# Storing q and k whole and splitting them beside the attention, with one plain gate moved ahead of the seven-product pairs

## The chip, the cores and the metric

The kernel runs on one core of one Trainium2 chip. The metric is device time in microseconds for one execution on that core; the kernel before was run three times, and its median is the number to beat. One further execution was taken with the hardware profiler, and every row quoted below is from it. Engines are named as the profile names them: PE is the matrix engine (PEld its weight loads), DVE the vector engine, ACT the scalar engine, POOL is GpSimd, SP the engine that issues most of the DMAs.

## The reference

One decoder block over 1024 tokens of width 1024, all in float32:

```python
h = rms_norm(x, g_pre_mix)
z = h @ w_in                 # q, k, v (1536 each), glu_in (2048), z_ga, z_gc (1024 each)
y_attn = dilated_attention_mixer(q, k, v, rel_bias_table, w_attn_out)
y_conv = conformer_conv_mixer(glu_in, ...)   # GLU, causal 31-tap depthwise conv, LayerNorm, swish, matmul
merged = sigmoid(z_ga) * y_attn + sigmoid(z_gc) * y_conv
x = x + rms_norm(merged @ w_mix_out, g_post_mix)
x = x + rms_norm(swiglu_ffn(rms_norm(x, g_pre_ffn), w_ffn_in, w_ffn_out), g_post_ffn)
```

The attention has three groups of eight heads (head size 64). A group with dilation d lets a token attend itself and up to 128 earlier tokens at distance d, with a learned bias by distance; the three groups' outputs are merged by their softmax denominators. A query block's score is `q . k / 8 + bias`.

## The kernel before

**Split products.** A float32 matrix product is made from rounded parts: an operand x becomes hi (x rounded to the matrix engine's format) and lo = x - hi, and a product is hi*hi + hi*lo + lo*hi, three matmuls of 128 x 512 per 128 rows of depth. hi is a copy on ACT, lo a subtraction on DVE or POOL (`wsplit` names which; it is changed from stage to stage).

**Units and pairs.** A *unit* (L288) is one 128 x 512 output at full depth: 24 matmuls. A *plain gate* is two units over the same weights. A *seven-product pair* (`winograd`, L316) makes four such outputs from two weight blocks with seven half-depth products of 12 matmuls each, 84 instead of 96; for it the weights are summed in four combinations (`quarters`, L191, steps 0 to 5: steps 1 and 3 are additions, the others splits), and the activations likewise, once (`quarter_sums`, L353). The outputs that need more than one product are taken from PSUM in callbacks f11, f12, f21, f22; the first, third and fourth products are copied out by ACT (L325, L330, L335), since their bank goes on accumulating or is summed with another.

**Order.** The program is written out in order by Python for all engines; each engine runs its own list in that order and waits on data. Every two or three matmuls a *tick* (L113) lets background generators emit a step: pieces of the weight splits, the convolution, normalisations. A *beat* (L131), one for each matmul of a unit or of v, lets the attention generator advance RATE steps (0.33 while v is made, 0.66 afterwards). Four such advances make one attention step (one block of 128 queries for two heads); eight steps make a head pair, twelve head pairs the attention.

**Stages.** (1) Start, and FIRST = 4 GLU blocks as units, with the quarter sums of the activations beside the last of them; what is not finished of them is forced at the first pair (L315, L336). (2) Pairs: 4 GLU, 4 of gate a, 3 of gate c, 12 of k with q. The depthwise convolution runs beside them on DVE, in PSUM banks of its own: 46 steps for each of 8 channel blocks, spaced by `CONV` (a list of ticks to skip after each step; L677, and another list for the q and k pairs, L1329). (3) v as plain products, with the LayerNorm of the convolution and then the attention beside. (4) LATE = 2 plain gates, the last two blocks of gate c (L1357), stored without their sigmoid, which follows at L1390. (5) The convolution's output product `co`, 16 units; its operand is loaded and split by `conv_split` (L1146), 8 splits for each half of the tokens, the first 8 of which must be out before the first unit (L1366). The rest of the attention and its merges run beside (4) and (5). (6) Attention output, mix, the FFN, its output.

**q and k.** `qk_pair` (L750) takes a pair of outputs, 128 channels (two heads) of k and of q. Every half (512 tokens) is brought into the group's order, split into hi and lo (`parts`, L772: a copy on ACT, L775 or L778, and a subtraction on DVE, L776 or L779; f21 does the same at L797 and L798), and stored to DRAM with one DMA for each part and head, 16 a pair (L769, L681). `stacks` (L805) loads a head's k as hi over lo on 128 partitions, and q's hi and lo on 64 each; `double` (L821) copies them to the other 64 partitions on POOL. A score block is then two matmuls (L967): both contract k's hi and lo in one go, once with q's hi in both halves and once with q's lo. `stacks` is called for the next head pair after the second step of the current one, and `double` after its sixth and seventh.

**Around a step.** In `attention` (L902) the scores of step s are followed by the exponentials of step s-1 on ACT (L980), the transposes of step s-3 on PE (L1003) with their split on ACT and DVE (L1008, L1009), and the products with v of step s-4 (L1024, L1026). v is split by `value_parts` (L854) in the third and fourth step.

Of the kernel before, what the change touches and what calls it, by code (L numbers as in the profile page):

```python
# [9 lines left out]
F32 = mybir.dt.float32  # L10
# [29 lines left out]
LATE = 2  # L40
# [18 lines left out]
class Build:  # L59
    def __init__(self, ctx, tc, aps):  # L60
# [12 lines left out]
        self.wsplit = self.nc.vector  # L73
# [117 lines left out]
    def quarters(self, i, c):  # L191
# [13 lines left out]
        elif c == 1:  # L205
            self.s12 = self.slot()
            add(self.s12[:, l], a21, a22, op=OP.add)
# [108 lines left out]
    def winograd(self, W, T, f11, f12, f21, f22):  # L316
# [18 lines left out]
        nc.scalar.copy(v1, V)  # L335
# [414 lines left out]
    def qk_pair(self, g, hp, job):  # L750
# [12 lines left out]
        def out(dst, part, hf, t):  # L763
            for h in range(2):
                d, x = dst[h][part * 64:part * 64 + 64], t[h * 64:h * 64 + 64]
                if dil == 1:
                    self.half_out(d, hf, x)
                else:
                    nc.sync.dma_start(d.rearrange("p (c h m) -> p c h m", c=dil, h=2)[:, :, hf],  # L769
                                      x.rearrange("p (c m) -> p c m", c=dil))  # L770

        def parts(y, hf, dst, scale):  # L772
            h = self.half(F32R)
            if scale is None:
                nc.scalar.copy(h, y)  # L775
                nc.vector.tensor_tensor(y.bitcast(F32R), y, f(h), op=OP.subtract)  # L776
            else:
                nc.scalar.activation(h, y, AF.Copy, scale=scale)  # L778
                nc.vector.scalar_tensor_tensor(y.bitcast(F32R), y, scale, f(h), op0=OP.mult, op1=OP.subtract)  # L779
            out(dst, 0, hf, f(h))  # L780
            out(dst, 1, hf, y)

        def row1(hf):
            def g(z, x):
                y = self.half()
                nc.vector.tensor_tensor(perm(y), nat(z), nat(x), op=OP.add)
                return lambda: parts(y, hf, dk, None)
            return g

        def f22(x, v):  # L790
            y = self.half()
            nc.vector.tensor_tensor(perm(y), nat(x), nat(v), op=OP.add)
            return lambda: parts(y, 1, dq, 0.125)

        def f21(x):
            h, l = self.half(F32R), self.half(F32R)
            nc.scalar.activation(perm(h), nat(x), AF.Copy, scale=0.125)  # L797
            nc.vector.scalar_tensor_tensor(perm(l), nat(x), 0.125, perm(f(h)), op0=OP.mult, op1=OP.subtract)  # L798
            out(dq, 0, 0, f(h))
            out(dq, 1, 0, f(l))  # L800
# [1033 lines left out]
```

## Time and profile before

| | |
|---|---|
| median of 3 runs | 1761.38 us (1760.35 to 1761.72) |
| the profiled execution | 1763.24 us |
| its span, first to last instruction | 1761.4 us |
| granted clock of the matrix engine, mean | 0.991 |
| bytes moved by DMA | 274.93 MB |

The median stands within a tenth of a per cent of the profiled execution. Busy time is the sum over instructions of an engine; on PE, where matmuls overlap, a row's mean duration (0.39 us for 128 x 512) is longer than the time from one start to the next. An idle entry in square brackets or behind the last bar of a group tells what the engine waited for just before the instruction. `out<-in` names tiles without their numbers: b are the 4 KB slots, c the 2 KB halves, p a PSUM bank. In the waits, `PE p L311 <- ACT c L325: 9.3, 2, 8.1` reads: PE at line 311 waited 9.3 us in all, in 2 places, 8.1 at the longest, for what ACT wrote at line 325.

### The profile page before, as it was taken

The page shows a single profiled execution, that of the slowest core. Times are in us where ns is not written, and L with a number is a line of the kernel's source. Part 1 is how long each engine was busy: PE and PEld are TensorE (multiplying, and loading weights), DVE is VectorE, ACT ScalarE, POOL GpSimd, SP SyncE. Part 2 cuts the span into 40 slices and gives each one's busy share as a digit, 9 for nine tenths or more (in the row PEclk, how much of TensorE's full clock was granted, in tenths as well). Part 3 has the DMA queues.
Part 4 walks back from the last instruction along what each step waited for, and adds up shares of the span by engine and source line. Part 5 has one row for each costly group of instructions (what it writes and reads, how often), then busy time and mean ns, then how long its engine had stood idle before and what let it go on. Part 6 is the DMA issues. An engine that isn't in the chain of part 4 may idle for free.

```text
span 1761.4 us, 24497 instructions
## 1 busy us (share of the span) xinstructions
PE 1714.6 (97%) x8698; PEld 1454.6 (83%) x8698; DVE 1245.9 (71%) x2207; ACT 792.3 (45%) x1549; POOL 478.5 (27%) x348
## 2 busy tenths in 40 slices
PE   8989999999999999999889999999999999999998
PEld 6768888888877999998678888878888888888886
DVE  6879988899896666556785675585665565667686
ACT  6333444444443576556542245633333333354453
POOL 0017778788774132233210130040000000000000
PEclk9989999999999999999899999999999999999999
DMA  4332433566667696669943742213233223395234
GB/s 161 123 133 102 138 131 126 148 191 170 166 166 196 220 283 163 170 185 273 280 155 120 275 164 87 102 39 123 90 121 113 90 103 113 132 337 178 97 129 150
DMA packets 185782, 274.93 MB, mean 156 GB/s; under 512 B 56113, under 2 KB 107948, under 8 KB 185660
## 3 DMA queue, kind: packets, MB, share of 16 engines
q1 hardware_dynamic: 185020, 272.74, 48.8%
q8 instruction: 68, 1.11, 0.3%
q10 hardware_dynamic: 576, 0.56, 0.1%
q14 instruction: 54, 0.44, 0.1%
q0 software_dynamic: 64, 0.07, 0.0%
HBM read 183.76 MB, written 94.28 MB: 158 GB/s over the span
## 4 chain that ended last, share of the span: by engine, by line
PE 84%; DVE 5%; DMA 4%; ACT 3%; issue 2%; POOL 1%; SPq 1%; DVEq 0%; ACTq 0%; POOLq 0%
PE p L311 13%; PE p L312 13%; PE p L313 13%; PE p L1718 12%; PE p L1452 5%; PE p L299 4%; PE p L295 4%; PE p L297 4%; PE p L885 2%; PE p L883 2%; PE p L887 2%; PE p L524 2%; PE p L967 2%; DMA b<-w_in 1%; PE p L1003 1%
## 5 line engine op out<-in xcount | busy, mean ns | idle before, releaser
L311 PE MATMUL p<-b,b 128*128 128x512 f32 x1204 | 470.8, 391 | 9.9 <-ACT c L325 9.3
L313 PE MATMUL p<-b,b 128*128 128x512 f32 x1204 | 470.5, 391 | 3.9 <-POOL b L188 3.9
L312 PE MATMUL p<-b,b 128*128 128x512 f32 x1204 | 470.1, 390 | 0.0
L311 PEld LDWEIGHTS p<-b,b 128*128 128x128 f32 x1204 | 226.9, 188 | 58.9 <-ACT c L325 10.3
L313 PEld LDWEIGHTS p<-b,b 128*128 128x128 f32 x1204 | 227.0, 189 | 52.9 <-POOL b L188 5.7
L312 PEld LDWEIGHTS p<-b,b 128*128 128x128 f32 x1204 | 227.1, 189 | 47.3
L187 ACT CAST b<-b 128x1024 fp32r<-128x1024 f32 x129 | 135.6, 1051 | 199.2 <-POOL b L208 73.4
L1718 PE MATMUL p<-b,b 128*128 128x512 f32 x924 | 209.6, 389 | 0.0
L1718 PEld LDWEIGHTS p<-b,b 128*128 128x128 f32 x924 | 173.4, 188 | 36.0
L188 POOL TENSOR_TENSOR b<-b,b 128x1024 fp32r<-128x1024 f32 x69 | 167.3, 2425 | 129.9 <-ACT b L187 117.6
L651 DVE SCALAR_TENSOR_TENSOR p<-b,par,p 128x511 f32<-128x511 f32 (+14 forms) x232 | 163.4, 737 | 0.0
L188 DVE TENSOR_TENSOR b<-b,b 128x1024 fp32r<-128x1024 f32 x60 | 73.4, 1223 | 127.3 <-ACT b L187 127.3
L295 PE MATMUL p<-b,b 128*128 128x512 f32 x368 | 150.5, 409 | 0.0
L299 PE MATMUL p<-b,b 128*128 128x512 f32 x368 | 148.9, 405 | 0.0
L297 PE MATMUL p<-b,b 128*128 128x512 f32 x368 | 148.8, 404 | 0.0
L885 PE MATMUL p<-b,b 128*128 128x256 f32 x384 | 114.0, 297 | 1.1 <-DVE b L181 1.1
L883 PE MATMUL p<-b,b 128*128 128x256 f32 x384 | 113.3, 295 | 0.0
L887 PE MATMUL p<-b,b 128*128 128x256 f32 x384 | 112.7, 293 | 0.0
L1086 DVE TENSOR_TENSOR b<-c,b 128x512 fp32r<-128x512 f32 x101 | 71.3, 706 | 40.5 <-ACT b L1085 40.1
L1086 DVE TENSOR_TENSOR b<-b,b 128x512 fp32r<-128x512 f32 x117 | 84.7, 726 | 17.3 <-ACT b L1085 15.3
L1085 ACT CAST b<-b 128x512 fp32r<-128x512 f32 x117 | 72.1, 619 | 44.5 <-PE p L1718 13.1
L1452 PE MATMUL p<-b,b 128*128 128x512 f32 x384 | 88.9, 391 | 0.0
(222 smaller groups left out, 2991.4 us busy)
## 6 DMA issues: line engine op xcount, KB each, us to landing
b<-w_in SPq DMA_DIRECT2D x53, 512.0 KB, 4.7
b<-w_fi SPq DMA_DIRECT2D x44, 512.0 KB, 4.7
dk<-c SPq DMA_DIRECT2D x96, 128.0 KB, 2.5
dq<-c SPq DMA_DIRECT2D x96, 128.0 KB, 2.4
b<-dq SPq DMA_DIRECT2D x48, 256.0 KB, 8.8
b<-dk SPq DMA_DIRECT2D x24, 512.0 KB, 7.6
dqS<-c SPq DMA_DIRECT2D x44, 256.0 KB, 2.2
b<-w_fo SPq DMA_DIRECT2D x44, 256.0 KB, 5.4
```

Of the source, the lines that this page charges most:

```text
L188: self.wsplit.tensor_tensor(lo, x, f(hi), op=OP.subtract)
L295: nc.tensor.matmul(ps, hi[:, s], a, start=kt == 0, stop=False)
L297: nc.tensor.matmul(ps, hi[:, s], b, start=False, stop=False)
L299: nc.tensor.matmul(ps, lo[:, s], a, start=False, stop=kt == nk - 1)
L311: nc.tensor.matmul(ps, hi[:, s], a, start=first and kt == 0, stop=False, skip_group_check=True)
L312: nc.tensor.matmul(ps, hi[:, s], b, start=False, stop=False, skip_group_check=True)
L313: nc.tensor.matmul(ps, lo[:, s], a, start=False, stop=kt == 3, skip_group_check=True)
L651: nc.vector.scalar_tensor_tensor(A[i][:, j:], src[i][:, :H - j], w[i], A[i][:, j:], op0=OP.mult, op1=OP.add)
L885: nc.tensor.matmul(o, a, lo[:, s], start=False, stop=False)
L1086: nc.vector.tensor_tensor(s[:, 512:512 + n], src, f(s[:, :n]), op=OP.subtract)
L1452: nc.tensor.matmul(banks[tt][nh], st, wt[:, nh * H:(nh + 1) * H], start=bool(kt == 0 and a), stop=bool(kt == KT - 1 and b))
L1718: nc.tensor.matmul(acc[t], x, y, start=first and e == 0, stop=last and e == 2, skip_group_check=True)
```

## The change

It has two parts and some settings around them.

*q and k.* `qk_pair` stores each half as it is, in float32, one DMA for both heads (4 a pair instead of 16). The factor 1/8 of q is applied in the callbacks and in the copy at L335. `stacks` loads k's 64 rows of a head twice, into both halves of a tile, and q's likewise (four DMAs a head instead of three). The new `parts` makes the operands for one head and one half of the tokens: ACT copies q (rounding it) to a second tile, POOL subtracts to leave q's lo; POOL rounds the upper half of k in place, rounds the lower half to a spare tile, and subtracts it from the lower half. It is called four times for a head pair, after the fourth to seventh step of the one before; `stacks` is called after the first step. For the first head pair the four calls stand 20 to 38 advances into the wait for the LayerNorm, which has at least 40 now.

*Gates.* LATE is 1 and EARLY is 1: gate c's last block is made as a plain gate after the GLU units and before the first pair; the number of pairs stays.

*Settings.* The first additions of the weight sums (`quarters`, step 1) go to an engine of their own, `wadd`, which is DVE at first, POOL beside the GLU and gate pairs, and DVE from the q and k pairs on; the second additions (step 3) stay with `wsplit`. The convolution keeps its first spacing through the q and k pairs. `conv_split` loads 4 halves ahead instead of 5.

```diff
-LATE = 2
+LATE = 1
+
+EARLY = 1
...
-        self.wsplit = self.nc.vector
+        self.wsplit = self.wadd = self.nc.vector
...
             self.s12 = self.slot()
+            add = self.wadd.tensor_tensor
             add(self.s12[:, l], a21, a22, op=OP.add)
...
-    def winograd(self, W, T, f11, f12, f21, f22):
+    def winograd(self, W, T, f11, f12, f21, f22, scale=1.0):
...
-        nc.scalar.copy(v1, V)
+        nc.scalar.activation(v1, V, AF.Copy, scale=scale)
...
-        def out(dst, part, hf, t):
-            for h in range(2):
-                d, x = dst[h][part * 64:part * 64 + 64], t[h * 64:h * 64 + 64]
-                if dil == 1:
-                    self.half_out(d, hf, x)
-                else:
-                    nc.sync.dma_start(d.rearrange("p (c h m) -> p c h m", c=dil, h=2)[:, :, hf],
-                                      x.rearrange("p (c m) -> p c m", c=dil))
-
-        def parts(y, hf, dst, scale):
...
+        def out(dst, hf, t):
+            if dil == 1:
+                self.half_out(dst, hf, t)
             else:
...
+                nc.sync.dma_start(dst.rearrange("p (c h m) -> p c h m", c=dil, h=2)[:, :, hf],
+                                  t.rearrange("p (c m) -> p c m", c=dil))
...
                 nc.vector.tensor_tensor(perm(y), nat(z), nat(x), op=OP.add)
-                return lambda: parts(y, hf, dk, None)
+                out(dk, hf, y)
...
-            nc.vector.tensor_tensor(perm(y), nat(x), nat(v), op=OP.add)
-            return lambda: parts(y, 1, dq, 0.125)
+            nc.vector.scalar_tensor_tensor(perm(y), nat(x), 0.125, nat(v), op0=OP.mult, op1=OP.add)
+            out(dq, 1, y)
...
-            h, l = self.half(F32R), self.half(F32R)
-            nc.scalar.activation(perm(h), nat(x), AF.Copy, scale=0.125)
-            nc.vector.scalar_tensor_tensor(perm(l), nat(x), 0.125, perm(f(h)), op0=OP.mult, op1=OP.subtract)
-            out(dq, 0, 0, f(h))
-            out(dq, 1, 0, f(l))
+            y = self.half()
+            nc.scalar.activation(perm(y), nat(x), AF.Copy, scale=0.125)
+            out(dq, 0, y)
...
         for h in range(2):
-            k, a, b = self.slot(F32R), self.slot(F32R), self.slot(F32R)
-            nc.sync.dma_start(f(a[top]), dq[h][top])
-            nc.sync.dma_start(f(b[low]), dq[h][low])
-            nc.sync.dma_start(f(k), dk[h])
-            ops.append((k, a, b))
+            k, q = self.slot(F32R), self.slot(F32R)
+            for x, d in ((q, 1), (k, 0)):
+                for r in (slice(0, 64), slice(64, 128)):
+                    nc.sync.dma_start(f(x[r]), self.d_qk[g, hp][d][h * 64:h * 64 + 64])
+            ops.append([k, None, q])
...
-    def double(self, p, hf):
...
+    def parts(self, p, h, c):
+        nc = self.nc
+        s, top, low = slice(c * H, (c + 1) * H), slice(0, 64), slice(64, 128)
+        o = p[2][h]
+        if c == 0:
+            o[1] = self.slot(F32R)
+        k, a, q = o
+        nc.scalar.copy(a[:, s], f(q[:, s]))
+        nc.gpsimd.tensor_tensor(q[:, s], f(q[:, s]), f(a[:, s]), op=OP.subtract)
+        t = self.half(F32R)
+        nc.gpsimd.tensor_copy(k[top, s], f(k[top, s]))
+        nc.gpsimd.tensor_copy(t[low], f(k[low, s]))
+        nc.gpsimd.tensor_tensor(k[low, s], f(k[low, s]), f(t[low]), op=OP.subtract)
...
-                    while after in self.gens or x is None:
+                    n = 0
+                    while after in self.gens or x is None or cur is None and n < 40:
...
+                        n += 1
+                        if cur is None and n in (20, 26, 32, 38):
+                            self.parts(nxt, n // 6 % 2 ^ 1, int(n > 30))
                         yield 0
-                    if cur is None:
-                        self.double(nxt, 0)
-                        self.double(nxt, 1)
...
-                if u in (6, 7) and nxt:
-                    self.double(nxt, u - 6)
+                if 3 < u < 8 and nxt:
+                    self.parts(nxt, u % 2, int(u > 5))
...
-                if u == 2 and order:
+                if u == 1 and order:
                     nxt = self.stacks(*order.pop(0))
...
-        x = [load(i) for i in range(5)]
+        x = [load(i) for i in range(4)]
...
+    early = [job(w_in[NGC + n]) for n in range(8 - EARLY, 8)]
...
+    def plain_gate(n, job):
+        w = B.weights(job)
+        s = B.slot()
+        for hf in range(2):
+            nc.scalar.copy(s[:, hf * H:(hf + 1) * H], B.unit(w, B.h_rhs(hf), KT))
+        nc.sync.dma_start(B.d_gc[n], s)
+
+    for n in range(EARLY):
+        plain_gate(8 - EARLY + n, early[n])
     B.first_sums(qs)
...
-        B.wsplit = nc.gpsimd
+        B.wsplit = B.wadd = nc.gpsimd
...
-    B.CONV = (1, 1, 0, 1)
+    B.wadd = nc.vector
...
     for n in range(LATE):
...
+        plain_gate(8 - LATE - EARLY + n, late[n])
```

34 lines of the change are left out of this document (7 added, 27 removed).

## The prediction

> **What bounds the kernel now.** I read the totals of the engines first, then busy time by stretches of 44 us, then PE's waits, then PE's timeline at the longest wait, and last the chain of waits.
>
> ```profile
> PE 1714.6 (97%) x8698; PEld 1454.6 (83%) x8698; DVE 1245.9 (71%) x2207; ACT 792.3 (45%) x1549; POOL 478.5 (27%) x348
> ```
>
> PE is busy for 97%, so the kernel can only get shorter where PE runs below its rate. The stretches say where (columns: length, busy us and count for PE, PEld, DVE, ACT, POOL, then granted clock, DMA share, GB/s):
>
> ```profile
> 88.00:132.00 44.00, 35.91 (x145) 28.38 (x145) 34.08 (x50) 17.19 (x27) 6.12 (x4) 0.88 0.37 133
> 132.00:176.00 44.00, 44.00 (x196) 36.44 (x195) 43.54 (x57) 17.52 (x26) 35.05 (x20) 1.00 0.29 102
> ...
> 440.00:484.00 44.00, 43.69 (x192) 35.69 (x192) 39.57 (x49) 18.09 (x27) 35.13 (x20) 1.00 0.62 164
> 484.00:528.00 44.00, 41.75 (x177) 34.03 (x177) 42.52 (x53) 17.85 (x25) 32.89 (x19) 0.96 0.67 166
> ...
> 836.00:880.00 44.00, 35.25 (x198) 29.71 (x197) 31.24 (x100) 24.00 (x82) 10.76 (x14) 0.88 0.95 283
> 880.00:924.00 44.00, 39.52 (x235) 33.23 (x234) 36.22 (x106) 22.67 (x74) 6.78 (x9) 0.96 0.47 153
> ```
>
> An undisturbed stretch of 512-wide products holds 196: 44/196 = 0.2245 us each. By that rate the stretch from 88 lost 51 products, 11.4 us; those from 440 and 484 lost 4 and 19, 5.2 us. The two from 836 mix widths; PE stood idle for 8.75 + 4.48 = 13.2 us in them. Who PE waited for:
>
> ```profile
> PE p L311 <- ACT c L325: 9.3, 2, 8.1
> ...
> PE p L313 <- POOL b L188: 3.9, 3, 2.3
> PE p L967 <- DMA b<-dk: 2.5, 1, 2.5
> ...
> PE p L967 <- POOL b L825: 1.1, 1, 1.1
> ```
>
> The longest is at the first seven-product pair:
>
> ```profile
> 108.06 0.39 PE L313 MATMUL p<-b,b 128*128 128x512 f32 x1
> 116.54 0.80 PE L311 MATMUL p<-b,b 128*128 128x512 f32 x1 [8.09 <-ACT c L325]
> 117.13 0.63 PE L312 MATMUL p<-b,b 128*128 128x512 f32 x1
> ```
>
> PE idles 8.09 us because the copy of the first product (L325) stands in ACT's queue behind the splits of the quarter sums; afterwards a product takes 0.63 instead of 0.39 us, the reduced clock (0.88 over the stretch). In the q and k stage the chain of waits runs for once not through PE:
>
> ```profile
> 443.30 1.67 SPq L769
> ...
> 447.72 4.08 DMA b<-w_in
> 451.88 1.06 ACT b L187
> ...
> 455.37 1.74 POOL b L207
> 457.19 1.30 POOL b L208
> ```
>
> There the weights are late: their load stands on SP behind the strided stores of q and k (L769), then GpSimd makes the sums.
>
> **The early gate.** Moving one plain gate from the late stage ahead of the pairs leaves the product count as it is. Its 48 products are 48 x 0.2245 = 10.8 us of work where PE now waits. The gate adds to the queues in question two splits on ACT and two on DVE and two copies out of PSUM; on ACT that is about 4 x 0.6 = 2.4 us (row L1085 below for a 512-wide copy). 8.09 + 2.4 = 10.5 is just under 10.8, and the sixteen ticks let the last quarter sums be issued before the pair instead of being forced inside it. I take -11 for this (idle and reduced clock together; ends -8, if 3 us of idle stay, and -11.4).
>
> **The q and k stage.** The rows that carry it:
>
> ```profile
> L188 POOL TENSOR_TENSOR b<-b,b 128x1024 fp32r<-128x1024 f32 x69 | 167.3, 2425 | 129.9 <-ACT b L187 117.6 <-issue 12.2
> L208 POOL TENSOR_TENSOR b<-b,b 128x512 f32<-128x512 f32 x23 | 32.5, 1412 | 1.8
> L651 DVE SCALAR_TENSOR_TENSOR p<-b,par,p 128x511 f32<-128x511 f32 (+14 forms) x232 | 163.4, 737 | 0.0
> L776 DVE TENSOR_TENSOR c<-c,c 128x512 fp32r<-128x512 f32 x24 | 39.3, 1638 | 14.0 <-ACT c L775 13.9
> L779 DVE SCALAR_TENSOR_TENSOR c<-c,c 128x512 fp32r<-128x512 f32 x12 | 13.8, 1154 | 2.0 <-ACT c L778 2.0
> L786 DVE TENSOR_TENSOR c<-p,c 128x512 f32<-128x512 f32 x24 | 22.9, 956 | 2.6 <-issue 2.6
> L798 DVE SCALAR_TENSOR_TENSOR c<-p,c 128x512 fp32r<-128x512 f32 x12 | 11.4, 948 | 0.5 <-ACT c L797 0.5
> L207 DVE TENSOR_TENSOR b<-b 128x512 f32<-128x512 f32 x20 | 13.7, 684 | 0.0
> L661 DVE TENSOR_TENSOR b<-p,c x8: 691/691/693, 170.8 to 545.5; 128x512 f32<-128x512 f32 x8
> ```
>
> Per pair (84 products, 18.9 us) stores fall from 16 to 4, so SP reaches the next weight load sooner, and none of the four waits for a split any more. GpSimd loses two additions, 2 x 1.41 = 2.8 us, exactly the two that end the chain above. DVE loses two subtractions of 1.638, one of 1.154 and one of 0.948 (8.25 us with the three sums of 0.956, L792 taken like L786) and gains the two additions at 0.684 each beside an idle GpSimd or 1.638 beside a busy one (L776 is such an operation, with both inputs in SBUF): 4.2 to 6.1 us. The convolution keeps its faster beat, 6 steps in 8 ticks instead of 4 in 7, so 21 steps in the pair's 28 ticks instead of 16: 3.7 us more at 0.737. Net -0.3 to +1.6 us of DVE per pair. DVE's idle time now is 4.4 us and 1.5 us in the two stretches, 1.9 and 0.6 us per pair, so the additions hide at the low end and cost up to 1.0 us per pair at the high one. The convolution's last block (L661) ends now at 545.5, near the stage's end; its 12 x 16 = 192 steps take 9 pairs at 21. So 0 to +9, taken +1, since at 43.54 of 44 us of DVE (stretch from 132) PE still ran 196 products. The late weights I take as cured: -5 (ends 0 and -5.2). ACT's 36 copies go from here; ACT is at 18 of 44 us, which is worth nothing. If DVE's cover is gone, the next thing late is q's sum, which PE needs before the last product of a pair.
>
> The Trainium skill ("SBUF — State Buffer", section "SBUF: two separate sides") says that DVE and GpSimd hold a shared port pair exclusively for a whole instruction when DVE has two SBUF inputs. Taken to the end, each moved addition would wait out a GpSimd subtraction of 2.425: 2 x 3.1 = 6.2 instead of at most 3.3 us, and the +1 would become 9 x 3.9 = 35, the time 1786. L776's 1.638 against 0.684 shows the effect, with 0.95 us of waiting and not 2.4; I give this end 2 in 100, inside the second rival.
>
> **The attention stage.** Halving the stored bytes happens in the stage before; here each head still reads 1 MB, in four DMAs instead of three. What is new runs on ACT and GpSimd:
>
> ```profile
> L860 POOL TENSOR_TENSOR b<-b,b 128x512 fp32r<-128x512 f32 x24 | 31.5, 1312 | 188.2 <-ACT b L859 149.4 <-PE p L1026 16.0 <-DMA b<-dq 14.8
> L1085 ACT CAST b<-b 128x512 fp32r<-128x512 f32 x117 | 72.1, 619 | 44.5 <-PE p L1718 13.1 <-DVE b L1573 12.6 <-DVE b L377 8.1
> ...
> b<-dq SPq DMA_DIRECT2D x48, 256.0 KB, 8.8
> ```
>
> ```profile
> 635.05 0.61 POOL L825 CAST b<-b 64x512 fp32r<-64x512 f32 x1 [4.32 <-DMA b<-dq]
> ...
> 641.04 0.61 POOL L825 CAST b<-b 64x512 fp32r<-64x512 f32 x1 [4.20 <-DMA b<-dq]
> ...
> 701.43 1.28 POOL L860 TENSOR_TENSOR b<-b,b 128x512 fp32r<-128x512 f32 x1 [16.66 <-ACT b L859]
> ...
> 725.23 1.29 POOL L860 TENSOR_TENSOR b<-b,b 128x512 fp32r<-128x512 f32 x1 [15.20 <-ACT b L859]
> ...
> 851.19 0.60 POOL L825 CAST b<-b 64x512 fp32r<-64x512 f32 x1 [6.30 <-DMA b<-dq]
> ...
> 855.70 0.61 POOL L825 CAST b<-b 64x512 fp32r<-64x512 f32 x1 [2.96 <-DMA b<-dq]
> ```
>
> A head pair takes 725.23 - 701.43 = 23.8 us, a step 3.0. Four calls of the new split cost GpSimd each a subtraction (1.31), two 64-row copies (0.61) and a 64-row subtraction that no row shows (0.61 to 1.31; nearer the first by its size): 3.1 to 3.8 us, 15 at most of 23.8, hidden. ACT gets 4 x 0.62 = 2.5 us of work, hidden too. The wait is what counts: ACT's copy waits for q in order, and behind it stand the exponentials and the copies of the transposed weights, for which PE waits. q is asked for after the first step instead of the second and used after the fourth (first head) and fifth instead of the sixth: 3 steps ahead instead of 4, 9 us against a median landing of 8.8. In quiet stretches nothing waits. Where GpSimd waits today (4.32 + 4.20 and 6.30 + 2.96) ACT will wait 3 us longer: 11.5 and 12.3 us. Exponentials run one step after the scores and transposes three after, so about 6 us are absorbed: 5.5 + 6.3 reach PE, less the 2.5 + 1.1 that PE loses at the same places today, and less some because the second head is asked as far ahead as before. I take +5 (ends 0, all absorbed, and +30, the four waits and 4 x 3.0 passed on whole). The first head pair is split well before its first scores: -1, the wait for L825.
>
> **The late stage.** With one gate less, 16 ticks instead of 32 cover the first eight activation splits; the first comes at tick 10, then one in 4, so two are done instead of six, and six are forced at once ahead of the first convolution-output unit.
>
> ```profile
> ACT b L1085 <- DMA c<-dact: 9.1, 3, 5.5
> ```
>
> ACT waits 9.1 us for these loads today. Forced together, the splits hold ACT until the last load lands; ends 0 (loads are early) and +12 (one landing of 8.8 in full, and 3 for a reduced clock as at 117). I take +4, near the 5.5 of the row less what PE has queued. Against that the second eight splits now come before the merges: -2 of the 13.2 us idle (ends 0 and -13). The 32 advances of the attention that rode on the moved gate (48 products at 0.66 each) ride on two more of the sixteen output units: nothing.
>
> The Trainium skill ("TensorE: Matmul & The Clock Gate", section "What's actually happening") halves PE's clock after an idle window of about 3.4 us; by that a forced wait of 4 costs 2 to 3 more, and one of 3 nothing more. The stretch from 484 shows 0.96 with no listed wait above 2.3, so here shorter gaps are also punished.
>
> **Edits at nothing:** the scale in L335's copy and in q's sum (same instruction and size), the gate's store, one pair of the FFN whose additions move to DVE (2 x 0.684 where DVE is 71% busy).
>
> **Sum:** -11 - 5 + 1 + 5 - 1 + 4 - 2 = -9. The profiled execution took 1763.2 us around a span of 1761.4; it becomes 1754.2. The median of the runs, 1761.4, lies 1.9 below the profiled execution, so 1752.
>
> **Rivals.** (1) *ACT waits for q in order* and passes all on: +30 instead of +5, 1777. It decides from 14 us passed to PE on. For: 8.8 us landing against 9 us of lead, DMA at 0.95 of its time from 836. Against: only two of twelve stacks wait seriously today. (2) *DVE becomes the bound* beside the faster convolution: no -5, +9 instead of +1, 1765. For: 42.52 of 44. Against: 43.54 without loss. (3) *The late stage clears*: no +4 and +5, and 13 instead of 2 of the idle time gone, 1752 - 20 = 1732. For: dact's loads no longer meet the merges. Against: they meet each other. (4) *The early gate only shifts the wait*: the queue it fills is the one PE waits for; no -11, 1763. For: 10.5 against 10.8. Against: the sums are issued over more ticks.
>
> **Numbers.** Forecast 0.50, rivals 0.17, 0.11, 0.15, 0.07. The range 1735 to 1768 leaves out the far half of (3) and most of (1). Its own range for the forecast is 1744 to 1757. What a measurement here can tell is 0.2%, 3.5 us. Faster: the forecast and (3), with a little of (2): 0.68. Within: parts of (2) and (4): 0.12. Slower: (1) and the rest of (2) and (4): 0.20.
>
> **What would show it.** Right: 196 products in every stretch from 88 to 132 with clock 1.00, no wait on L188 in the q and k stage, the convolution's last block near 490. Wrong: PE waiting for the copy of transposed weights or for an exponential where ACT's idle time ends on a DMA of q; DVE near 44 of 44 with PE waiting for q's sum; a long wait at the first output unit. If the first stretch keeps its gap, the largest term falls and with it the forecast.

## The result and the profile after

The changed kernel takes 1790.81 us (median of 4 runs, 1787.94 to 1791.52) against 1761.55 for the kernel before beside it: ratio 1.0159, interval 1.0140 to 1.0178, some 28 us slower where 9 faster was forecast. Its profiled execution took 1791.15 us around a span of 1789.4. First the busy time in the same stretches as before (columns as there), with the totals of the page:

```profile
PE 1729.5 (97%) x8698; PEld 1467.9 (82%) x8698; DVE 1216.2 (68%) x2183; ACT 797.3 (45%) x1561; POOL 561.6 (31%) x420
```

```profile
88.00:132.00 44.00, 42.57 (x186) 34.15 (x185) 33.27 (x50) 18.64 (x30) 4.92 (x3) 1.00 0.45 161
...
440.00:484.00 44.00, 43.13 (x191) 35.39 (x190) 41.61 (x59) 15.69 (x21) 28.00 (x16) 1.00 0.39 122
484.00:528.00 44.00, 43.85 (x194) 36.00 (x193) 20.81 (x23) 14.97 (x21) 28.59 (x15) 1.00 0.46 135
...
836.00:880.00 44.00, 31.25 (x160) 26.74 (x159) 27.15 (x69) 23.91 (x71) 20.50 (x18) 0.77 0.88 231
880.00:924.00 44.00, 39.27 (x225) 33.23 (x223) 30.75 (x103) 24.51 (x87) 31.61 (x32) 0.92 0.69 207
```

The two gains are there. The stretch from 88 has 186 products instead of 145: 41 x 0.2245 = 9.2 us. Those from 440 and 484 have 385 together instead of 369: 3.6 us. DVE is busy for 20.8 of 44 us there, where it was busy for 42.5. The loss shows in the attention: 160 products instead of 198 in the stretch from 836, with the clock at 0.77 instead of 0.88 (products of several widths, so the count is a first sign only). Who PE waited for:

```profile
PE p L1022 <- DVE c L1005: 12.5, 14, 2.2
PE p L1020 <- DVE b L1027: 12.3, 1, 12.3
PE p L1020 <- POOL b L817: 8.0, 1, 8.0
...
PE p L314 <- ACT c L328: 2.9, 2, 1.4
```

The long wait at the first pair (8.1) is gone. New are two long ones and many short ones. In the changed kernel L816 to L821 are the new split, L963 the scores, L966 the addition of the bias into a shared half, L1004 and L1005 the split of the transposed weights, L1020 and L1022 the products with v, L1027 their sum out of PSUM. The many short waits end on DVE's L1005; what DVE waits for, from 640 to 960 us, stands in its own waits (the kernel before has no such row):

```profile
DVE c L1005 <- POOL b L821: 29.1, 13, 4.3
...
DVE c L966 <- POOL b L821: 10.2, 8, 2.2
```

39 us of waiting for the last instruction of the new split, though neither L1005 nor L966 reads anything that it makes. One of these places in the timelines of GpSimd and of DVE (start, us, engine, line):

```profile
821.75 1.29 POOL L817 TENSOR_TENSOR b<-b,b 128x512 fp32r<-128x512 f32 x1
822.98 0.61 POOL L819 CAST b<-b 64x512 fp32r<-64x512 f32 x1
823.65 0.61 POOL L820 CAST c<-b 64x512 fp32r<-64x512 f32 x1
824.34 1.26 POOL L821 TENSOR_TENSOR b<-b,c 64x512 fp32r<-64x512 f32 x1
```

```profile
825.64 0.42 DVE L1005 TENSOR_TENSOR c<-p,c 128x256 fp32r<-128x256 f32 x1 [4.33 <-POOL b L821]
```

GpSimd's subtraction ends at 825.60 and DVE starts at 825.64. What DVE needs is not the result but the place: L1005 writes into a shared half (`c`), and, as I read it, the half that is next in the row of 13 is the spare tile that L820 wrote and L821 reads last. One call of the split takes GpSimd from 821.75 to 825.68, 3.9 us, and four calls follow one another in order, so a half can be held for many microseconds by an engine that is behind. The run own_12 below tests this reading.

The two long waits, in the timeline of ACT:

```profile
633.84 0.62 ACT L816 CAST b<-b 128x512 fp32r<-128x512 f32 x1 [7.14 <-DMA b<-dq]
...
635.35 0.35 ACT L1004 CAST c<-p 128x256 fp32r<-128x256 f32 x1
...
638.09 0.62 ACT L816 CAST b<-b 128x512 fp32r<-128x512 f32 x1 [2.39 <-DMA b<-dq]
...
851.20 1.17 ACT L1081 CAST b<-c 128x512 fp32r<-128x512 f32 x2 [12.12 <-DMA c<-dact]
```

From 626.7 ACT waits in order for q of the second head pair, whose parts are made during the first. Behind it stand exponentials and the copy of the transposed weights (L1004), which ends at 635.7; PE goes on at 635.85. That is PE's 8.0 us; GpSimd's L817, which the row names, ends at the same moment and isn't what PE reads. From 839 ACT waits 12.1 us for the convolution's activation, in the splits forced ahead of the first output unit; DVE's half of these splits (L1082) waits for ACT's, and behind it stands the L1027 that PE waits for: 12.3 us. SP's timeline shows why those loads (L1149) were late:

```profile
822.52 9.56 SPq L1149 DMA_DIRECT2D c<-dact  x2
832.17 1.13 SPq L801 DMA_DIRECT2D b<-dq  x2
833.36 1.23 SPq L801 DMA_DIRECT2D b<-dk  x2
834.63 1.23 SPq L801 DMA_DIRECT2D b<-dq  x2
835.91 1.23 SPq L801 DMA_DIRECT2D b<-dk  x2
...
841.51 8.42 SPq L1149 DMA_DIRECT2D c<-dact  x6
```

SP itself stands at L1149 from 822.5, two loads in 9.6 us, then issues the eight loads of the next head pair (L801), and only at 841.5 the six that ACT needs. Its waits from 780 to 870 us say what it stood for, again a half of DVE's:

```profile
SPq L1149 <- DVE c L1005: 15.2, 4, 9.2
```

### The profile page after: what moved, and what is told of

Read it like the earlier page. It is cut to its first block, busy times and chain, and to the rows that moved or that the text cites. A ratio compares the mean times of both kernels' runs of the same rounds, so it can differ in the third digit from the quotient of the medians.

```text
span 1789.4 us, 24469 instructions
## 1 busy us (share of the span) xinstructions
PE 1729.5 (97%) x8698; PEld 1467.9 (82%) x8698; DVE 1216.2 (68%) x2183; ACT 797.3 (45%) x1561; POOL 561.6 (31%) x420
## 4 chain that ended last, share of the span: by engine, by line
PE 68%; DVE 4%; POOL 2%; ACT 2%; DMA 2%; issue 2%; SPq 0%; DVEq 0%; POOLq 0%; ACTq 0%
PE p L1720 12%; PE p L314 10%; PE p L315 10%; PE p L316 10%; PE p L1454 5%; PE p L302 3%; PE p L300 3%; PE p L298 3%; PE p L880 3%; PE p L882 2%; PE p L878 2%; PE p L963 2%; PE p L999 1%; PE p L1022 1%; PE p L1020 1%
## 5 line engine op out<-in xcount | busy, mean ns | idle before, releaser
L314 PE MATMUL p<-b,b 128*128 128x512 f32 x1204 | 469.0, 390 | 4.7 <-ACT c L328 2.9
L316 PE MATMUL p<-b,b 128*128 128x512 f32 x1204 | 468.5, 389 | 0.0
L315 PE MATMUL p<-b,b 128*128 128x512 f32 x1204 | 468.5, 389 | 0.0
L1720 PE MATMUL p<-b,b 128*128 128x512 f32 x924 | 209.6, 389 | 0.0
L298 PE MATMUL p<-b,b 128*128 128x512 f32 x368 | 153.9, 418 | 0.0
L300 PE MATMUL p<-b,b 128*128 128x512 f32 x368 | 153.2, 416 | 0.0
L302 PE MATMUL p<-b,b 128*128 128x512 f32 x368 | 151.8, 412 | 0.0
L1082 DVE TENSOR_TENSOR b<-c,b 128x512 fp32r<-128x512 f32 x101 | 73.9, 735 | 46.1 <-ACT b L1081 45.8
L1005 DVE TENSOR_TENSOR c<-p,c 128x256 fp32r<-128x256 f32 (+1 forms) x96 | 52.2, 544 | 71.6 <-ACT c L1004 36.8
L1082 DVE TENSOR_TENSOR b<-b,b 128x512 fp32r<-128x512 f32 x117 | 85.2, 730 | 21.2 <-ACT b L1081 19.2
```

Source lines behind the costliest of these rows:

```text
L298: nc.tensor.matmul(ps, hi[:, s], a, start=kt == 0, stop=False)
L300: nc.tensor.matmul(ps, hi[:, s], b, start=False, stop=False)
L302: nc.tensor.matmul(ps, lo[:, s], a, start=False, stop=kt == nk - 1)
L314: nc.tensor.matmul(ps, hi[:, s], a, start=first and kt == 0, stop=False, skip_group_check=True)
L315: nc.tensor.matmul(ps, hi[:, s], b, start=False, stop=False, skip_group_check=True)
L316: nc.tensor.matmul(ps, lo[:, s], a, start=False, stop=kt == 3, skip_group_check=True)
```

## The experiments

The kernels below ran each beside runs of the kernel before on the same chip. Differences below are taken between ratios and turned to time with 1761 us; so the changed kernel stands at +28.0. The theories by letter, as the expectations use them: **L**, the moved gate costs in the late stage what it wins early; **S**, the spare half that GpSimd holds among the shared ones; **Q**, ACT's waits for q in order. Later ones (F, W, P, O, N) are named where they are tried.

| kernel | median us | ratio (interval) | us against before |
|---|---|---|---|
| changed | 1790.81 | 1.0159 (1.0140 to 1.0178) | +28.0 |
| gate_alone | 1750.27 | 0.9939 (0.9922 to 0.9956) | -10.7 |
| gate_back | 1790.86 | 1.0177 (1.0162 to 1.0192) | +31.2 |
| own_spare | 1778.96 | 1.0104 (1.0089 to 1.0119) | +18.3 |
| q_on_pool | 1815.19 | 1.0312 (1.0296 to 1.0327) | +54.9 |
| five_ahead | 1790.22 | 1.0163 (1.0147 to 1.0178) | +28.7 |
| q_later | 1787.55 | 1.0145 (1.0130 to 1.0160) | +25.5 |
| own_all | 1784.42 | 1.0125 (1.0108 to 1.0142) | +22.0 |
| k_short | 1767.79 | 1.0035 (1.0021 to 1.0049) | +6.2 |
| u2_own | 1777.98 | 1.0092 (1.0073 to 1.0111) | +16.2 |
| u2_short | 1758.44 | 0.9988 (0.9978 to 0.9998) | -2.1 |
| k_dve | 1805.84 | 1.0253 (1.0237 to 1.0268) | +44.6 |
| gate_wadd | 1771.15 | 1.0055 (1.0040 to 1.0070) | +9.7 |
| own_12 | 1769.53 | 1.0054 (1.0039 to 1.0069) | +9.5 |
| u2_12 | 1763.90 | 1.0019 (1.0010 to 1.0028) | +3.3 |
| gate_43 | 1776.11 | 1.0091 (1.0074 to 1.0108) | +16.0 |
| gate_45 | 1752.44 | 0.9957 (0.9942 to 0.9972) | -7.6 |
| u2_45 | 1765.17 | 1.0026 (1.0015 to 1.0038) | +4.6 |
| u2_first | 1762.02 | 1.0002 (0.9993 to 1.0012) | +0.4 |

### The two parts of the change apart

*gate_alone*: the kernel before with one plain gate early, and nothing of q and k.

```diff
-LATE = 2
+LATE = 1
+EARLY = 1
...
+    early = [job(w_in[NGC + n]) for n in range(8 - EARLY, 8)]
...
+    for n in range(EARLY):
+        plain_gate(8 - EARLY + n, early[n])
     B.first_sums(qs)
```

> The kernel before with nothing but one plain gate moved from the late stage ahead of the first pair. Theory L: about -9 at the first pair and +20 or more at the output units, 1772 to 1780 us. Theories S and Q: the late stage is as before, 1750 to 1754.

*gate_back*: the changed kernel with both plain gates late.

```diff
-LATE = 1
+LATE = 2
 
-EARLY = 1
+EARLY = 0
```

> The changed kernel with both plain gates in the late stage again (EARLY 0, LATE 2); q and k stay whole in DRAM. Theory L (the late stage lost the gate that covered the loads and splits of the convolution's activations): the 8 us wait at the first pair comes back (about +9), the 12 us wait at the first output unit and the reduced clock after it go (about -20 to -25), so 1775 to 1780 us. Theories S (the spare half that GpSimd holds in the new split makes DVE and ACT wait for GpSimd) and Q (ACT waits in order for the loads of q) do not need the gate: only the +9 comes, about 1800.

The early gate alone wins 10.7 us, and its late stage pays little for it; L falls as a general cause. In the changed kernel the same edit is worth 3.2 at most (the intervals overlap), since there the one late gate leaves ACT with the forced splits (12.1 us on dact), while gate_back shows 1.3 us on dact and loses the time in small waits instead (18.7 us of PE on DVE's L1005, where the changed kernel has 12.5). So the q and k part costs 28.0 + 10.7 = 38.7 us where the prediction had +2 for all that was not the early gate. PE's own times say where: gate_alone and the changed kernel have the same stages in the same order, and from the first product of v to the first of the mix the one takes 454.6 us (558.3 to 1012.9) and the other 493.2 (556.7 to 1049.9), 38.6 more. From the first pair to the first product of v it is 2.5 less (442.6 against 445.1). All that follows looks for these 38.7.

### The spare half

*own_spare*: the spare tile gets two buffers of its own, for which one of the 44 slots goes.

```diff
-NSLOT = 44
+NSLOT = 43
...
-        t = self.half(F32R)
+        self.uid += 1
+        t = self.pool.tile([128, 512], F32R, tag="t", bufs=2, name=f"t{self.uid}")
```

> The changed kernel, but the spare half of the new split comes from two buffers of its own (one 4 KB slot fewer for the rest), so no half that DVE or ACT write next is ever held by GpSimd. Theory S: the waits of DVE on L821 (17 us in all in the late stage) go, 10 to 15 us less, 1776 to 1781. Theory L: at most 3 us less. Theory Q: no change.

*q_on_pool*: q's rounding copy moves from ACT to GpSimd, which makes each call of the split longer there and takes ACT's wait away.

```diff
-        nc.scalar.copy(a[:, s], f(q[:, s]))
+        nc.gpsimd.tensor_copy(a[:, s], f(q[:, s]))
```

> The changed kernel with the rounding copy of q on GpSimd instead of ACT, so ACT never waits for a load of q. Theory Q: the 8 us wait of PE at the start of the second head pair goes, and smaller ones with it, 1778 to 1783. Theory L: only that one wait goes or shrinks, 1782 to 1788. Theory S: GpSimd is longer busy with each half of a head pair and holds the spare half longer, so the waits on it grow, 1790 to 1800.

9.7 us won by the one, 26.9 lost by the other. In q_on_pool PE's wait of 8.0 us is gone, and DVE's wait for the half that L821 frees grows from 29.1 to

```profile
DVE c L1005 <- POOL b L821: 59.7, 17, 13.0
```

A slower GpSimd makes DVE wait longer, as S has it; as the main cause, Q falls.

*own_12*: one own buffer, taken from the shared halves (12 left), with all 44 slots. *gate_43*: the slot's price by itself, on gate_alone.

```diff
-NHALF = 13
+NHALF = 12
...
-        t = self.half(F32R)
+        self.uid += 1
+        t = self.pool.tile([128, 512], F32R, tag="t", bufs=1, name=f"t{self.uid}")
```

```diff
-NSLOT = 44
+NSLOT = 43
```

> The changed kernel with one buffer of its own for the spare tile, taken from the 13 shared halves (12 left), and all 44 slots. Theory S (sharing costs: a half that GpSimd reads last comes round in the row of halves that DVE, ACT and SP take in order): the waits on L821 go as with two own buffers, and without the slot that those cost, 1779.0 - 8 = 1771 (1768 to 1776). Rival N (the number of halves is what is short): twelve are worse than thirteen, 1788 to 1796.

> The early gate alone (1750.3) with 43 slots instead of 44: the price of the slot that the spare tile's own buffers took, apart from anything with q and k. If the 8 us that PE loses more at 120 to 160, 360 to 400 and 1120 to 1200 us with 43 slots are the slot's: 1756 to 1760. If they come with q and k: 1750 to 1752, and then the spare tile's own buffers saved 12 us and not 20.

own_12 wins 18.5 us over the changed kernel with *fewer* shared halves, so not their number was short (N falls): what cost was that GpSimd held one of the row. DVE's waits from 640 to 960 us hold no row with GpSimd any more; these are all its rows of over 5 us:

```profile
DVE c L1006 <- ACT c L1005: 37.9, 63, 1.5
DVE c L967 <- PE p L964: 21.7, 51, 0.9
DVE b L1028 <- PE p L1023: 12.8, 32, 0.8
DVE b L1083 <- ACT b L1082: 12.8, 2, 12.5
DVE b L1074 <- ACT b L1073: 5.8, 3, 2.6
```

The slot is dearer than I thought: on gate_alone it costs 26.7 us instead of the 6 to 10 expected. In the changed kernel it costs less: own_spare stands 8.8 above own_12, and u2_own, below, 12.9 above u2_12. So own_spare paid in part for what it won. *gate_45* and *u2_45* (45 slots, two halves less) ask the reverse.

```diff
-NSLOT = 44
-NHALF = 13
+NSLOT = 45
+NHALF = 11
```

> The early gate alone (1750.3) with two shared halves less and one slot more (45 and 11, the same space). If slots are what is short (43 cost 26 us): 1742 to 1749. If halves are short as well (DVE and ACT wait for them around the attention): 1752 to 1765.

> The version with the spare tile's own buffer and the old places (1763.9) with two shared halves less (10) and 45 slots. If what is left of the loss is the third slot for each head, which the loads and weights beside the attention wait for: 1752 to 1760. If ten halves are too few: 1766 to 1780. If neither: 1761 to 1766, and the rest is ACT's wait for q at the second head pair (PE 5.2 us) and what follows it.

Neither gains: -7.6 against -10.7 and 4.6 against 3.3, intervals that overlap. One slot more, paid for with two halves, gains nothing; one slot more by itself was not tried.

### The two long waits

*five_ahead* loads five halves ahead of the convolution's splits instead of four; *q_later* splits the second head pair's operands at the sixth and seventh step; *own_all* does both on own_spare.

```diff
-        x = [load(i) for i in range(4)]
+        x = [load(i) for i in range(5)]
...
-            if i < 12:
-                x.append(load(i + 4))
+            if i < 11:
+                x.append(load(i + 5))
```

```diff
-                if 3 < u < 8 and nxt:
+                if 3 < u < 8 and nxt and cur[:2] != [0, 0]:
                     self.parts(nxt, u % 2, int(u > 5))
+                if 5 < u < 8 and cur[:2] == [0, 0]:
+                    for h in range(2):
+                        self.parts(nxt, h, u - 6)
```

> The changed kernel with five instead of four halves loaded ahead of the activation splits. Theory F (the forced splits before the first output unit hold ACT for 12.1 us because their last loads start late): the wait of ACT on dact shrinks by half or more and the time falls by 5 to 9 us, to 1782 to 1786. Theory S (what costs is the shortage of shared halves): one more half is held by a load, DVE and ACT wait for halves as long or longer, and the time stays or rises, 1789 to 1797, even if the wait on dact gets shorter.

> The changed kernel with the splits for the second head pair moved from the fourth to seventh step of the first one to its sixth and seventh (two each); nothing else moves. Theory W (ACT's 7.1 us wait on q at 626 us is passed on to PE as 8.0, and one late place is all there is to it): the wait goes, PE loses 1 to 3 us instead of 10.6 between 620 and 640, and the time falls by 7 to 9, to 1782 to 1784. Rival (the operands are then late for the first scores of the second pair): PE waits for GpSimd at the scores instead, 4 to 8 us, and the time is 1787 to 1792.

> The changed kernel with three edits together: the spare tile from two buffers of its own (1779.0 by itself), the second pair's splits later, five halves ahead. If the three losses are separate places, they add: 1779 - 8 - 5 = 1766 (1762 to 1769). If the next late thing takes over where one is cured, 1771 to 1779. Either way it should stay above the 1750.3 of the gate alone if GpSimd's longer work itself costs.

All three miss. With five ahead ACT still waits 11.6 us for dact, for the loads ahead are not what is late; the last ones are. q_later takes the 8.0 us of PE away but wins only 2.5 in all: the waits on L1005 rise to 14.3 and those on the forced splits to 13.3. own_all is no better than own_spare alone. F and W, each wait as a place of its own, fall.

*u2_12* and *u2_own* put loads and splits at the old places (loads after the second step, splits at the sixth and seventh), on own_12 and on own_spare:

```diff
-                if 3 < u < 8 and nxt:
-                    self.parts(nxt, u % 2, int(u > 5))
+                if 5 < u < 8 and nxt:
+                    for h in range(2):
+                        self.parts(nxt, h, u - 6)
...
-                if u == 1 and order:
+                if u == 2 and order:
```

> The changed kernel with the spare tile from buffers of its own (1779.0 by itself) and with the old places: loads for the next head pair after the second step, splits at the sixth and seventh step (two each). Theory O (order on SP: the eight loads asked for one step earlier stand on SP ahead of the last six loads of the convolution's activation, which therefore start at 841 us instead of 816 as in the gate alone, and ACT's splits wait 12 us for them; and q is read too early in the second head pair): both waits go, 1779 - 6 - 8 = 1765 (1760 to 1769). Rival (GpSimd has less time for the same work, so its results are late at the first scores of a pair): PE waits for GpSimd at the scores, 1775 to 1790.

> As own_12, and with the old places of the loads (after the second step) and splits (sixth and seventh step). Theories S and O together: own_12 less the two waits, near the 1758.4 of the kernel that leaves k's low part out: 1758 to 1766. Rival P (GpSimd's time for k's low part costs by itself, wherever its spare tile lies): 1772 to 1780, as with two own buffers and 43 slots.

Theory O says that the step between the loads is what counts, by their order on SP. SP's timeline in own_12 and in u2_12, at the same place:

```profile
818.97 1.13 SPq L801 DMA_DIRECT2D b<-dq  x2
820.15 1.23 SPq L801 DMA_DIRECT2D b<-dk  x2
821.42 1.52 SPq L801 DMA_DIRECT2D b<-dq  x2
822.99 1.23 SPq L801 DMA_DIRECT2D b<-dk  x2
...
828.35 7.70 SPq L1150 DMA_DIRECT2D c<-dact  x6
```

```profile
822.40 3.93 SPq L1151 DMA_DIRECT2D c<-dact  x6
...
829.06 1.78 SPq L801 DMA_DIRECT2D b<-dq  x2
831.17 1.12 SPq L801 DMA_DIRECT2D b<-dk  x2
```

The six loads now go ahead of the eight, 6 us sooner, and PE's longest wait at the forced splits falls from 14.1 to 4.5 us. u2_12 wins 6.2 us over own_12, as O expects. The places of the loads and those of the splits were moved together, so their shares are not told apart; PE's wait for the second head pair's q falls too, from 8.1 to 5.2. u2_own has the shorter waits too (8.3 us of ACT on dact, 4.1 at the longest, instead of 11.8), but its 2.1 us over own_spare lie within the intervals: with 43 slots other waits took the time.

*u2_first* moves the second pair's splits one step later still.

```diff
-                if 5 < u < 8 and nxt:
+                late = int(cur[:2] == [0, 0])
+                if 5 + late < u < 8 + late and nxt:
                     for h in range(2):
-                        self.parts(nxt, h, u - 6)
+                        self.parts(nxt, h, u - 6 - late)
```

> The version with the spare tile's own buffer and the old places (1763.9), with the splits for the second head pair one step later (after the seventh and eighth step of the first pair), all others as there. If the waits of ACT for q at 628 to 636 us (3.9 and 3.7, PE behind them 5.2) are what is left to cure: 1757 to 1760. If GpSimd is then late for the first scores of the second pair, the wait only moves from ACT to PE: 1762 to 1767.

PE's wait there falls from 5.2 to 2.7 us, the time by 3.0, with intervals that overlap a little; it is no clear gain.

### GpSimd's own time, and DVE's

*k_short* and *u2_short* round k only, on the changed kernel and with the old places; they leave k's low part out of the scores, so they only tell of time.

```diff
-        t = self.half(F32R)
-        nc.gpsimd.tensor_copy(k[top, s], f(k[top, s]))
-        nc.gpsimd.tensor_copy(t[low], f(k[low, s]))
-        nc.gpsimd.tensor_tensor(k[low, s], f(k[low, s]), f(t[low]), op=OP.subtract)
+        nc.gpsimd.tensor_copy(k[:, s], f(k[:, s]))
```

> The changed kernel with k only rounded, all 128 rows in one copy; the lower half's rounding to the spare tile and its subtraction are left out, so k's low part is missing in the scores. Takes no spare half and 48 x (0.61 + 1.28) = 91 us off GpSimd. Theory S (only the spare half costs): the same as with the spare tile from buffers of its own, 1776 to 1781. Theory P (GpSimd's time itself costs, by operands that are late, by v's parts queued behind it or by what DVE does beside it): clearly below, 1762 to 1773.

> The changed kernel with k only rounded (k's low part is missing in the scores; 1767.8 by itself) and with the old places of the loads and splits. Theory O: the two remaining waits (7.8 on GpSimd at the second pair, 12.5 at the first output unit against 6.3 in the gate alone) go: 1767.8 - 8 - 6 = 1754 (1748 to 1758), about the gate alone. Rival (the waits come from the number of loads and bytes in these stretches, not from their order): 1764 to 1769.

k_short wins 21.8 us, 3.3 more than own_12; u2_short stands 5.4 below u2_12. So beyond the sharing GpSimd's 91 us for k's low part cost 3 to 5 us (P, small). And u2_short against k_short wins 8.3 by the old places alone, as O expects.

*k_dve*: own_spare with the last subtraction on DVE.

```diff
-        nc.gpsimd.tensor_tensor(k[low, s], f(k[low, s]), f(t[low]), op=OP.subtract)
+        nc.vector.tensor_tensor(k[low, s], f(k[low, s]), f(t[low]), op=OP.subtract)
```

> The changed kernel with the spare tile from buffers of its own, and the subtraction that leaves k's low part on DVE instead of GpSimd. Theory P (GpSimd's own time costs the 11 us between 1779.0 and 1767.8, since what it makes comes late): GpSimd loses 48 x 1.28 = 61 us, the time falls by 4 to 8, to 1771 to 1775. Rival (DVE is where time is short around the attention, and its queue is in order): DVE gets 48 times 0.4 to 0.7 us and waits for GpSimd's rounding inside its queue: 1780 to 1795.

26 us slower than own_spare. What DVE waits for, from 600 to 960 us:

```profile
DVE b L822 <- POOL t L821: 69.8, 42, 11.2
```

DVE now has to wait for GpSimd's rounding inside its own ordered list: again a slower engine stops it, this time for data and not for a place.

*gate_wadd*: gate_alone with the change's engine for the first additions of the weight sums, and q and k split before DRAM as before.

```diff
+            add = self.wadd.tensor_tensor
             add(self.s12[:, l], a21, a22, op=OP.add)
...
-        B.wsplit = nc.gpsimd
+        B.wsplit = B.wadd = nc.gpsimd
...
     B.CONV = (1, 1, 0, 1)
+    B.wadd = nc.vector
```

> The kernel before with the early gate (1750.3) and with the change's engine for the first additions of the weight sums (DVE in the q and k pairs); q and k stay split before DRAM and the convolution keeps its slower beat there. The part of the 5 us won in the q and k stage that comes from the additions: 1746 to 1749 if the late weights were GpSimd's, 1750 to 1751 if it was the stores ahead of the loads on SP, 1752 to 1757 if DVE has no room for them.

20.4 us slower than gate_alone, far above what I gave it. The stretch from 440, the only wait of PE that its list has from 330 to 580 us, and the rows of the additions (by shape, 396 to 528 us), in gate_wadd:

```profile
440.00:484.00 44.00, 40.32 (x170) 32.53 (x169) 40.85 (x52) 16.91 (x23) 26.36 (x14) 0.96 0.61 160
```

```profile
PE p L314 <- DVE c L795: 17.3, 11, 2.5
```

```profile
L210 DVE TENSOR_TENSOR b<-b 128x512 f32<-128x512 f32 x6 | 12.2, 2030 | 2.5 <-DMA b<-w_in 2.5
L211 DVE TENSOR_TENSOR b<-b,b 128x512 f32<-128x512 f32 x6 | 6.9, 1158 | 0.2
```

and in the changed kernel:

```profile
L211 DVE TENSOR_TENSOR b<-b,b 128x512 f32<-128x512 f32 x8 | 9.7, 1211 | 0.3
...
L210 DVE TENSOR_TENSOR b<-b 128x512 f32<-128x512 f32 x7 | 5.7, 810 | 1.6 <-DMA b<-w_in 1.6
```

170 products in a stretch where the changed kernel has 191 and gate_alone 195. L795 is q's sum, for which PE waits eleven times. So the additions go to DVE at no such cost only because the splits of q and k have left it.

## Why the prediction was wrong, step by step

- **The early gate, -11**: right. 9.2 us by the products of its stretch, 10.7 when it is the only edit.
- **The late weights, -5, and DVE, +1**: right in direction. 3.6 us by the products of the two stretches against the kernel before, and 2.5 against gate_alone from the first pair to v; the last step of the convolution's last block starts at 491.6 us in DVE's timeline, instead of 545.5, as foretold (490). The price of 0.684 to 1.638 for a moved addition holds the means, 0.81 and 1.21, but its reason was wrong: I took L776's mean of 1.638 for a wait of 0.95 at each meeting. Of the 22 moved additions between 330 and 560 us, 17 took 0.68 or 0.69, since no GpSimd subtraction ran when they began; the other five waited out the one that ran (1.10 to 2.77, in the last section). So the price was low because meetings were few, and in that the sum had luck. The rival by which DVE becomes the bound needs the q and k splits to stay on it: gate_wadd shows it, at +20.4.
- **The split's work on GpSimd, "3.1 to 3.8 us, 15 at most of 23.8, hidden"**: this is the step that failed, and the largest. The size was about right, 3.9 us a call and 16 a head pair. "Hidden" was wrong, for I asked only whether GpSimd has time for it, and not what it holds meanwhile: the spare tile is one of the 13 halves that DVE and ACT take in order, and they stop at it until GpSimd has read it. That is 18.5 us, shown by own_12, and 26.9 more when GpSimd is slower still (q_on_pool).
- **Forced splits, +4, up to +12**: 12.3 us at PE, the upper end, and for another reason than I gave. I counted the loads against their landing time, not against SP's queue: `stacks` was moved ahead of them there, with eight DMAs instead of six, and SP stood waiting for a half besides. Against the 6.3 us in all for which PE waits at the same operation in gate_alone it is some 6 too many, which is what the old order wins back (6.2 in u2_12, 8.3 in u2_short).
- **ACT waits for q, +5**: the place was foreseen (the second head pair, at 635 us in the profile before), but of the 6 us that I had absorbed nothing was: ACT's first wait, 7.14 us, became 8.0 of PE and a halved clock after it. Its second, 2.39, stopped PE for no time that the profile lists. At 851, where I expected the other half of it, no wait for q came.
- **Second splits before the merges, -2**: not seen. **First head pair split early, -1**: a slip. The 1.1 us of PE on L825 are gone, but they stood at 643 us, at the first scores of the second head pair, and the term for q had already taken them off; at the first pair there was nothing to win. The 32 advances on the output units, "nothing", can't be separated.
- **The rivals**: that ACT passes all waits for q on would have been 1777, and the time was beyond it, by a mechanism that stood in no rival. The late stage did not clear, and the early gate did not merely shift its wait.

The 38.7 us between the changed kernel and gate_alone, in the order in which the runs take them off: 18.5 the sharing of the spare half (own_12), 6.2 the order of loads and splits (u2_12), 5.4 GpSimd's time for k's low part (u2_short, which also has its thirteenth half back). 8.6 remain between u2_short and gate_alone, and PE's own times put them, and a little more, in the same stage: 465.7 us from the first product of v to the first of the mix (556.4 to 1022.1) against 454.6, 11.1 of cost, less what the q and k stage gains. The trace puts part of it where ACT still waits for q in the first pair (in u2_12 PE waits 5.2 us there, in gate_alone no longer than 0.7 for anything between 600 and 700 us); the rest I can't attribute, and u2_first did not settle it. The parts are not independent either: q_later, own_all and u2_own show that one of them taken away gives the others more.

gate_alone beats both kernels, 1750.27 us.

## What to carry to other kernels

When an edit gives work to an engine with time to spare, ask not only whether the work fits but which buffers it holds until it is done, and which engine takes the next buffer of that row: a late reader of one shared tile stops every writer behind it, whatever the share of busy time says. When loads are asked for earlier, write down what they now stand ahead of in their queue. And a move that is free in the whole change (the additions on DVE) may be so only because another part of it made the room.

## What the runs showed of the hardware

GpSimd's subtraction of 64 rows takes as long as one of 128. The groups by shape from 640 to 800 us in the changed kernel:

```profile
L821 POOL TENSOR_TENSOR b<-b,c 64x512 fp32r<-64x512 f32 x27 | 35.0, 1295 | 2.2
L817 POOL TENSOR_TENSOR b<-b,b 128x512 fp32r<-128x512 f32 x27 | 34.8, 1288 | 2.0 <-ACT b L816 0.5
```

The prediction had left this open from 0.61 to 1.31. The Trainium skill ("GPSIMD Engine Reference", section "2. Architecture") gives each of GpSimd's eight cores 16 fixed partitions for ordinary work, by which half the rows save nothing; the rows agree.

In the changed kernel, between 330 and 560 us, a moved addition that began on DVE while a GpSimd subtraction was running ended 0.55 us after that subtraction. One of the five that did so, in the timelines of GpSimd and of DVE:

```profile
357.21 2.72 POOL L190 TENSOR_TENSOR b<-b,b 128x1024 fp32r<-128x1024 f32 x1 [0.32 <-POOL b L670]
```

```profile
357.71 2.77 DVE L211 TENSOR_TENSOR b<-b,b 128x512 f32<-128x512 f32 x1
```

The subtraction ends at 359.93 and the addition at 360.48; the other four show the same distance. The Trainium skill ("SBUF — State Buffer", section "SBUF: two separate sides") would have an addition wait out a whole GpSimd subtraction, 3.1 in all by the estimate of the prediction if both begin together; these five agree.

The clock stays halved long after PE is at work again. Stretches around the wait at the forced splits, PE starting again at 853.6:

```profile
841.00:843.00 2.00, 0.34 (x2) 0.03 (x1) 0.00 (x0) 0.00 (x0) 0.00 (x0) 1.00 1.02 229
...
845.00:847.00 2.00, 0.00 (x0) 0.00 (x0) 0.00 (x0) 0.00 (x0) 0.00 (x0) 0.85 1.01 47
847.00:850.00 3.00, 0.00 (x0) 0.00 (x0) 0.00 (x0) 0.00 (x0) 0.00 (x0) 0.50 0.85 143
...
854.00:858.00 4.00, 3.79 (x13) 3.21 (x13) 3.66 (x11) 4.00 (x12) 2.07 (x2) 0.50 1.03 409
858.00:862.00 4.00, 4.00 (x16) 3.53 (x15) 1.18 (x7) 3.27 (x12) 3.86 (x5) 0.50 0.22 82
862.00:866.00 4.00, 4.00 (x16) 3.41 (x15) 3.75 (x7) 0.91 (x3) 3.86 (x4) 0.50 0.44 133
866.00:870.00 4.00, 4.00 (x25) 3.58 (x25) 3.73 (x10) 2.24 (x8) 3.78 (x5) 0.89 0.82 254
```

It falls some 5 us after PE stopped (841.3) and comes back at about 866.9, after 13 us in which PE was busy nearly throughout. If PE ran at half its rate for these 13 us, that is another 6.5 of work, so by this estimate the wait of 12.3 cost about 19. The Trainium skill ("TensorE: Matmul & The Clock Gate", section "What's actually happening") has the full clock back after at least one busy window of about 3.4 us; here it took nearly four times as long.
